# Two-layer decoder trunk on one core: SBUF padded so that matmul operands begin at one place modulo 512 bytes, Strassen sums kept over passes, banks named

## The chip, the core and the metric

The kernel runs on one core of one Trainium2 chip, alone. The metric is the device time of one execution in microseconds. Before the change it is 2031.8 us, the median of three runs (2031.58 to 2032.2).

## What is computed

Two layers over 256 tokens of width 2048, everything in float32. Layer 0 is a gated short convolution, layer 1 multi-head latent attention; each is followed by a squared-ReLU MLP of width 8192, and each half of a layer ends with a normalised residual. Cut to what the change touches:

```python
D_MODEL = 2048; SEQ = 256; DEPTH = 2; D_FF = 4 * D_MODEL
ALPHA = (2 * DEPTH) ** 0.25

def short_conv_mixer(x, w_in, conv_w, w_out):
    bcu = x @ w_in
    gate_b, gate_c, u = jnp.split(bcu, 3, axis=-1)
    v = gate_c * u
    ...
    return (gate_b * y) @ w_out

def sq_relu_mlp(x, w1, w2):
    return jnp.square(jax.nn.relu(x @ w1)) @ w2

for layer in range(DEPTH):
    if layer < N_A:
        mix = short_conv_mixer(h, conv_w_in[layer], conv_w[layer], conv_w_out[layer])
    else:
        ...
        mix = mla_mixer(...)
    h = layer_norm(ALPHA * h + mix, ln_g[layer, 0], ln_b[layer, 0])
    h = layer_norm(ALPHA * h + sq_relu_mlp(h, mlp_w1[layer], mlp_w2[layer]),
                   ln_g[layer, 1], ln_b[layer, 1])
```

## The kernel before

**Numbers in two parts.** A float32 matrix is split into a high and a low part that TensorE multiplies in float32r, three products for one (high x high, high x low, low x high). Weights come from DRAM as raw tiles of 128x1024, on SP's queue; ScalarE copies the high part (L116), VectorE subtracts to get the low part (L117). `take` gives the next weights and prepares those up to five tiles ahead (`LOOK`), so the order of loads, splits and their place among the other work is fixed in the program. An activation tile holds high and low parts side by side.

**Products of 512 columns.** `products` (the MLP's up-projection) and `lagged` (the other wide products) hold a 128x128 block of weights in TensorE and move the activations past it: per 128 rows of the contraction one matmul against 512 columns (L192, high weights against both parts of x) and one against 256 (L196, low weights against x's high part). In the trace's names `out<-moving,held` this is `ps_u<-xhl,hi`. `opening` does the first four products of the kernel in the same way, four banks in turn, in growing runs of chunks. The down-projection is the other way round: `dot` (L276 to L278) holds a 128x128 piece of the hidden activations and moves 512 columns of weights past it, three times.

**The MLP** (`mlp`) runs over the hidden width in eight passes (q = 0 to 7) of eight chunks. A pass computes its eight products of up-projection, whose outputs `hidden` reads out (ScalarE copies one half, VectorE adds the other, L333), squares and splits into `h` (L337, L338). Then come the down-projections of the pass, of four column blocks n of 512 by two halves t of 128 tokens, added up in the SBUF tile `acc` by `put` (copied in pass 0, L577, added later, L581). Pass 0 takes its inputs before the norm is finished and corrects after; pass 7 ends in `to_wide` (layer 0: transposes, L665, and the next norm) or in `to_out` (layer 1: last norm with the vectors `gbt`, and stores).

**Fast passes.** In passes 1 to 6 the column blocks 0 and 1 are done by Strassen's scheme: seven products in place of eight, each of 4 steps of three matmuls, 84 matmuls in all (`down_fast`, tile `ps_f`). Blocks 2 and 3 then take 96 plain matmuls (`down`, `ps_d`). Both layers together have twelve fast passes. The sums of activations that the scheme needs are formed by VectorE (L605 to L608) into the tile `forms`; sums of weights by `prepare` (L149 to L155), the last one in a tile `t4`. After the seven products `combine` folds them into `acc`, with eleven additions by VectorE and a copy by ScalarE, the scratch `vu` being two of the raw tiles.

**Banks.** PSUM has eight banks, taken in turn by every output: four of the pool `pmm`, four of a second pool.

**Places in SBUF.** These are the places at which the built program puts the tiles that TensorE reads, as byte address modulo 512, before and after the change. All lie in the same 128 partitions.

| tile | before | after |
|---|---|---|
| weights, high and low (`hi`, `lo`, and the Strassen sums `hi_t`, `lo_t`) | 384 | 384 |
| `h`, `lat` (tag c) | 384 | 384 |
| `forms`, `kqv` (tag a2) | 0 | 384 |
| `t4` | 256, one buffer | 384, two buffers |
| first input `xhl_a`, chunks 0 to 7 (a1) | 384 | 384 |
| first input `xhl_a`, chunks 8 to 15 (a2) | 0 | 384 |
| `xhl`, `z`, `oT` (tag b) | 128 | 128 |
| `kpe` | 256 | 384 |

In the down-projection `h` and `forms` are held and the weights and `t4` (named `t` in the trace) move; in the other products the weights are held.

Of the kernel before, what the change touches and what calls it, by code (L numbers as in the profile page):

```python
# [16 lines left out]
P = 128  # L17
W = 256 + 2
T = 256
# [31 lines left out]
def trunk(ctx: ExitStack, tc: tile.TileContext, xT, vecs, w_first, w_in, w_out, w_kv, w_q, w_uk, w_uv,  # L51
# [9 lines left out]
    pmm = ctx.enter_context(tc.tile_pool(name="pmm", bufs=4, space=PS))  # L61
# [12 lines left out]
    def mlp_stream(l):  # L74
        out = []
        for q in range(NQ):
            out += halves(w1[l, q * QC:(q + 1) * QC])
            lead = 0
            if q in FAST:
                out += [(w2f[l, q, j, 0], w2f[l, q, j, 1]) for j in range(QC // 2)]  # L80
                lead = 2
            out += halves(w2[l, q, lead:])
        return out
# [6 lines left out]
    class Banks:  # L90
# [4 lines left out]
        @classmethod  # L95
        def open(cls, name):
            st = ExitStack()
            cls.more, cls.count = st.enter_context(tc.tile_pool(name=name, bufs=4, space=PS)), 0
            return st
# [6 lines left out]
        @classmethod  # L106
        def next(cls):
            cls.count += 1
            return cls.more if cls.more is not None and cls.count % 8 >= 4 else pmm
# [70 lines left out]
    def psum(name):  # L180
        return Banks.next().tile([P, 512], F32, tag="mm", name=name)
# [83 lines left out]
    def products(n, x, turned=None):  # L265

        for i in range(n):
            w = take()
            ps = psum("ps_u")
            mm_run([(w, ps)], x, 0, NC, NC, turned=None if i else turned)  # L270
            yield ps
# [8 lines left out]
    def held(x, t):  # L280

        return [x[:, o + t * P:o + (t + 1) * P] for o in (0, T)]
# [5 lines left out]
    def down(x, put, n):  # L288

        ps = [psum("ps_d") for _ in range(2)]  # L290
        for j in range(len(x) // 2):
            w, = take(1)
            for kk in range(2):
                k = 2 * j + kk
                for t in range(2):
                    dot(ps[t], wide_rows(w, kk), held(x[k], t), k == 0, k == len(x) - 1)
        for t in range(2):
# [13 lines left out]


    FACTORS = (("4", "22", "T4"), ("2", "12", "21"), ("3", "S4", "22"), ("1", "11", "11"),
               ("6", "S2", "T2"), ("7", "S3", "T3"), ("5", "S1", "T1"))

    def down_fast(x, forms):

        ps = {p: psum(f"ps_f{p}") for p, _, _ in FACTORS}
        n = len(x) // 2
        for j in range(n):  # L320
            b, = take(1)
            a = {"11": held(x[2 * j], 0), "12": held(x[2 * j + 1], 0), "22": held(x[2 * j + 1], 1)}
            for i in range(4):
                a[f"S{i + 1}"] = [forms[:, j, o, i * P:(i + 1) * P] for o in range(2)]
            for p, l, r in FACTORS:
                dot(ps[p], b[r], a[l], j == 0, j == n - 1)
        return ps
# [14 lines left out]
    cos_t = const.tile([P, T], F32, name="cos_t")  # L342
    sin_t = const.tile([P, T], F32, name="sin_t")
    mask_t = const.tile([P, 3 * P], F32, name="mask_t")
# [9 lines left out]

    def late_constants():
        nc.sync.dma_start(id_t, ident)
        nc.sync.dma_start(cos_t, cosT)
        nc.sync.dma_start(sin_t, sinT)
        nc.sync.dma_start(mask_t, mask)
# [145 lines left out]
    xres = act.tile([P, NC, T], F32, tag="xres", name="xres")  # L505
# [47 lines left out]
    late_constants()  # L553
# [3 lines left out]
    def mlp(idx, ln, blocks, fast, begin=None, extra=None):  # L557
# [24 lines left out]

        for q in range(NQ):
# [5 lines left out]
            if q == NQ - 1 and begin:  # L589
                begin()  # L590
            pair = []

            def hidden(m, ps, evac, *func):
                f = tmp.tile([P, T], F32, tag="fh", name="fh", bufs=3)
# [5 lines left out]
                pair.append(f)  # L600
                if forms is not None and m % 2:
                    (a11, a21), (a12, a22) = ((v[:, :P], v[:, P:]) for v in pair[-2:])
                    sf = fast.tile([P, 4, P], F32, tag="sf", name="sf")
                    s1, s2, s3, s4 = (sf[:, i, :] for i in range(4))
                    nc.vector.tensor_tensor(s1, a21, a22, ALU.add)  # L605
                    nc.vector.tensor_tensor(s3, a21, a11, ALU.subtract)
                    nc.vector.tensor_tensor(s2, s1, a11, ALU.subtract)
                    nc.vector.tensor_tensor(s4, a12, s2, ALU.subtract)  # L608
                    split(forms[:, m // 2, 0, :], forms[:, m // 2, 1, :], sf.rearrange("p i c -> p (i c)"))

            if q == 0:
                for m in range(QC):
# [12 lines left out]
                    if m > 0:  # L625
                        normal()
                acc = act.tile([P, 2, D], F32, tag="a1", name=f"acc{idx}")
            else:
                for m, ps in enumerate(products(QC, xhl, turned=None if q == NQ - 1 and begin else TURNED)):
                    hidden(m, ps, whole)  # L630

# [3 lines left out]
            if q in FAST:  # L635
# [6 lines left out]
    def combine(put, p):  # L642

        put(0, 1, p["4"])
        put(0, 0, p["2"])
        put(1, 0, p["3"])
        v, u = (raws.tile([P, 2, BW], F32, tag="raw", name="vu")[:, i, :] for i in range(2))
        put(0, 0, p["1"])
        nc.scalar.copy(v, p["1"])
        nc.vector.tensor_tensor(v, v, p["6"], ALU.add)  # L650
        nc.vector.tensor_tensor(u, v, p["7"], ALU.add)
        put(1, 0, v)
        put(0, 1, u)
        put(1, 0, p["5"])
        put(1, 1, u)
        put(1, 1, p["5"])
# [23 lines left out]
    def prepare_all():  # L680
        for k in range(NC):
            ln.prepare(k)

    with tc.tile_pool(name="fast1", bufs=1) as fast:
        mlp(1, before, to_wide, fast, begin=prepare_all)


    with tc.tile_pool(name="att", bufs=1) as ap:
        lat = act.tile([P, 2 * NK, 2 * T], F32R, tag="c", name="lat")
        chl, qhl = ([lat[:, k, :] for k in range(o, o + NK)] for o in (0, NK))  # L690
        kpe = ap.tile([P, 2, T], F32, name="kpe")
# [6 lines left out]
        def rope(dst, src, rows):  # L698

            a = tmp.tile([P, T], F32, tag="sq", name="ropea")  # L700
            b = tmp.tile([P, T], F32, tag="nu", name="ropeb")
# [201 lines left out]
    def turn_residual(block, n):  # L903
        if 0 <= n < NB:
            for t in range(2):
                ps = psum("turned")
                for j in range(4):
                    nc.tensor.transpose(ps[:, j * P:(j + 1) * P], xres[:, 4 * n + j, t * P:(t + 1) * P], id_t)
                nc.vector.scalar_tensor_tensor(block(n, t), ps, ALPHA, block(n, t), ALU.mult, ALU.add)

    def to_out(block, put, h):
        gbt = act.tile([P, NB, 2 * BW], F32, tag="b", name="gbt")
        for n in range(NB):
            nc.gpsimd.dma_start(gbt[:, n, :], gb[n].partition_broadcast(P))
# [148 lines left out]
```

## Time and profile before

| what | before |
|---|---|
| median of the runs | 2031.8 us |
| the profiled execution, its own time | 2031.86 us |
| its span | 2030.0 us |
| granted TensorE clock | 1.0 |
| TensorE, VectorE, ScalarE busy | 2022.8, 1637.1, 1186.2 us |
| DMA, mean over the span | 190 GB/s |

The span runs from the first to the last instruction that the profiler saw; the time of an execution has some 2 us more around it. PE is TensorE, PEld its weight loads (they overlap the matmuls), DVE VectorE, ACT ScalarE, POOL GpSimd, SP the engine that issues most DMAs. Matmuls are pipelined: the duration given for one (390 ns for 512 columns) is longer than the distance from its start to the next, so the sum of durations in a group is not its share of the time, and times of stretches are taken from start to start.

### The profile page before, as it was taken

To read this page: it belongs to the slowest core of one execution; us is meant where nothing else is said; L and a number is where in the kernel's file an instruction comes from. 1 tells how busy PE (TensorE), PEld (TensorE's weight loads), DVE (VectorE), ACT (ScalarE), POOL (GpSimd) and SP (SyncE) were. 2 spreads that over 40 slices of the span, in tenths; PEclk is the share of its full clock that TensorE was granted. 3 is DMA by queue.
4 is the path that set the end of the run, shared out by engine and by line. 5 is a ranking of instruction groups with operands and counts; after the bars stand their busy time and mean duration, and the time that the engine had idled before them with its cause. 6 is when DMAs were issued, how large, how long until landed. Compare 5 with 4: busy or idle time off the path is not lost.

```text
span 2030.0 us, 30192 instructions
## 1 busy us (share of the span) xinstructions
PE 2022.8 (100%) x11240; PEld 1763.4 (87%) x11240; DVE 1637.1 (81%) x2559; ACT 1186.2 (58%) x1849; POOL 4.5 (0%) x25
## 2 busy tenths in 40 slices
PE   9999999999999999999999999999999999999998
PEld 8888888988888888888889998898888888888886
DVE  7667677778898988989788978776889898898966
ACT  6444445676566565655656655566656656565661
POOL 0000000000000000000000000000000000000000
PEclk9999999999999999999999999999999999999999
DMA  8666666564746557465654544656474664746573
GB/s 307 209 191 187 188 190 193 162 210 138 251 148 216 193 170 256 145 229 174 232 176 153 177 129 137 195 168 205 136 240 155 213 204 164 250 143 221 190 228 121
DMA packets 106851, 385.32 MB, mean 190 GB/s; under 512 B 11856, under 2 KB 12752, under 8 KB 106448
## 3 DMA queue, kind: packets, MB, share of 16 engines
q1 hardware_dynamic: 105984, 381.17, 57.9%
q0 software_dynamic: 576, 2.10, 0.3%
q8 instruction: 88, 1.44, 0.3%
q14 instruction: 59, 0.48, 0.1%
q10 hardware_dynamic: 144, 0.13, 0.0%
HBM read 381.25 MB, written 2.10 MB: 189 GB/s over the span
## 4 chain that ended last, share of the span: by engine, by line
PE 99%; DMA 0%; DVE 0%; issue 0%; SPq 0%; ACT 0%; DVEq 0%
PE ps_u L192 20%; PE ps_l L192 13%; PE ps_u L196 11%; PE ps_d L276 7%; PE ps_d L277 7%; PE ps_d L278 7%; PE ps_l L196 7%; PE ps_f L278 4%; PE ps_f L276 4%; PE ps_f L277 4%; PE ps_w L226 1%; PE ps_w L224 1%; PE ps_w L225 1%; PE ps_g L226 1%; PE ps_g L224 1%; PE ps_g L225 1%
## 5 line engine op out<-in xcount | busy, mean ns | idle before, releaser
L117 DVE TENSOR_TENSOR lo<-raw,hi 128x1024 fp32r<-128x1024 f32 x710 | 858.7, 1222 | 271.5 <-ACT hi L116 199.9
L116 ACT CAST hi<-raw 128x1024 fp32r<-128x1024 f32 x710 | 740.9, 1050 | 428.4 <-DMA raw<-in_w_dram 134.6
L192 PE MATMUL ps_u<-xhl,hi 128*128 128x512 f32 x1792 | 621.3, 391 | 0.0
L196 PE MATMUL ps_u<-xhl,lo 128*128 128x256 f32 x1792 | 500.1, 280 | 0.0
L192 PEld LDWEIGHTS ps_u<-xhl,hi 128*128 128x128 f32 x1792 | 334.4, 187 | 71.9
L196 PEld LDWEIGHTS ps_u<-xhl,lo 128*128 128x128 f32 x1792 | 339.2, 189 | 1.7
L276 PE MATMUL ps_d<-hi,h 128*128 128x512 f32 x640 | 249.9, 390 | 0.0
L277 PE MATMUL ps_d<-lo,h 128*128 128x512 f32 x640 | 249.3, 390 | 0.0
L278 PE MATMUL ps_d<-hi,h 128*128 128x512 f32 x640 | 249.2, 389 | 0.0
L192 PE MATMUL ps_l<-xhl_a,hi 128*128 128x512 f32 x704 | 244.1, 393 | 0.0
L196 PE MATMUL ps_l<-xhl_a,lo 128*128 128x256 f32 x704 | 195.5, 280 | 0.0
L192 PEld LDWEIGHTS ps_l<-xhl_a,hi 128*128 128x128 f32 x704 | 132.2, 188 | 29.8
L278 PEld LDWEIGHTS ps_d<-hi,h 128*128 128x128 f32 x640 | 120.2, 188 | 25.2
L276 PEld LDWEIGHTS ps_d<-hi,h 128*128 128x128 f32 x640 | 120.2, 188 | 25.0
L277 PEld LDWEIGHTS ps_d<-lo,h 128*128 128x128 f32 x640 | 120.2, 188 | 24.6
L196 PEld LDWEIGHTS ps_l<-xhl_a,lo 128*128 128x128 f32 x704 | 131.9, 188 | 0.2
L597 ACT ACTIVATE fh<-fh 128x256 f32<-128x256 f32 x112 | 46.5, 415 | 89.2 <-DVE fh L333 89.1
L116 ACT CAST hi_t<-raw_t 128x1024 fp32r<-128x1024 f32 x48 | 50.6, 1054 | 55.5 <-DVE raw_t L149 30.5
L192 PE MATMUL ps_l<-z,hi 128*128 128x512 f32 x240 | 82.4, 391 | 0.0
L226 PE MATMUL ps_w<-xd,hi 128*128 128x258 f32 x256 | 72.7, 285 | 0.0
L224 PE MATMUL ps_w<-xd,hi 128*128 128x258 f32 x256 | 72.6, 284 | 0.0
L225 PE MATMUL ps_w<-xd,lo 128*128 128x258 f32 x256 | 72.4, 283 | 0.0
(253 smaller groups left out, 3185.1 us busy)
## 6 DMA issues: line engine op xcount, KB each, us to landing
raw<-in_w_dram SPq DMA_DIRECT2D x416, 512.0 KB, 4.3
raw<-in_w2f_dram SPq DMA_DIRECT2D x96, 512.0 KB, 3.5
raw<-in_w_in_dram SPq DMA_DIRECT2D x88, 512.0 KB, 3.8
raw<-in_w_out_dram SPq DMA_DIRECT2D x32, 512.0 KB, 3.6
raw<-in_w_o_dram SPq DMA_DIRECT2D x32, 512.0 KB, 4.0
raw<-in_w_kv_dram SPq DMA_DIRECT2D x10, 512.0 KB, 3.6
raw<-in_w_q_dram SPq DMA_DIRECT2D x8, 512.0 KB, 4.4
raw<-in_w_uk_dram SPq DMA_DIRECT2D x8, 512.0 KB, 4.6
```

Of the source, the lines that this page charges most:

```text
L116: nc.scalar.copy(hi, src)
L117: nc.vector.tensor_tensor(lo, src, hi.bitcast(F32), ALU.subtract)
L192: nc.tensor.matmul(ps, w[blk // 8][0][:, blk % 8, :], x, start=first, stop=False)
L196: nc.tensor.matmul(ps[:, :T], w[blk // 8][1][:, blk % 8, :], x[:, :T], start=False, stop=last)
L224: nc.tensor.matmul(ps[:, :W], hi, x[k][:, :W], start=k == 0, stop=False)
L225: nc.tensor.matmul(ps[:, :W], lo, x[k][:, :W], start=False, stop=False)
L226: nc.tensor.matmul(ps[:, :W], hi, x[k][:, W:], start=False, stop=k == NC - 1)
L276: nc.tensor.matmul(ps, x[0], w[0], start=first, stop=False)
L277: nc.tensor.matmul(ps, x[0], w[1], start=False, stop=False)
L278: nc.tensor.matmul(ps, x[1], w[0], start=False, stop=last)
L597: nc.scalar.activation(f, f, AF.Relu)
```

## The change

1. Tiles are declared once at the start in a set order with pads between them (`at_...`), so that the held and the moving operands begin where the table above says. The DMA scratch shrinks from 16384 to 4096 bytes to make room.
2. In the fast passes the seven products are no longer folded after each pass. Three of them ("2", "3", "4") are added to their own block of `acc`, four ("1", "5", "7", "6") to a tile `sums`, copied there in the first fast pass; `fold` does the combining once, one step after each of the first products of pass 7.
3. `down_fast` becomes `first_pair` and `fast_products`; the seven factors are taken in another order, and `t4` has two buffers.
4. PSUM banks are named: the up-projection of passes 1 to 7 uses banks 0 and 1 alone, the Strassen products 2 to 7 and 0, the plain blocks 1, 2 and 3, 4, the transposed residual 5 and 6. Other outputs take turns as before.
5. In the fast passes `h` is split for two chunks at once.
6. The next norm's preparation in layer 0, which was done all together at the start of pass 7, takes two chunks after each product of that pass (the first chunk in pass 0). The transposed residual in layer 1 is added between block 2 and block 3, not before block 3's banks are taken.
7. The rotary tables and the mask are loaded on SP's queue behind the first MLP instead of after the convolution; `gbt` is loaded by SP instead of GpSimd.

```diff
-    pmm = ctx.enter_context(tc.tile_pool(name="pmm", bufs=4, space=PS))
+    pmm = ctx.enter_context(tc.tile_pool(name="pmm", bufs=1, space=PS))
+    xres = act.tile([P, NC, T], F32, tag="xres", name="xres")
+    for tag, columns in (("c", 4096), ("pad0", 64), ("b", 8256), ("a1", 4128), ("pad1", 96), ("a2", 4128), ("pad2", 96)):
+        act.tile([P, columns], F32, tag=tag, name=f"at_{tag}")
+    small.tile([P, 32], F32, tag="pad", name="at_pad", bufs=1)
...
-        f = state["fast"].tile([P, 2, BW], F32R, tag="t4", name=f"t4_{i}")
+        f = state["fast"].tile([P, 2, BW], F32R, tag="t4", name=f"t4_{i}", bufs=2)
...
-    def psum(name):
-        return Banks.next().tile([P, 512], F32, tag="mm", name=name)
+    def psum(name, bank=None):
+
+        bank = Banks.next() if bank is None else bank
+        return (pmm if bank < 4 else Banks.more).tile([P, 512], F32, tag=f"mm{bank}", name=name)
...
-    FACTORS = (("4", "22", "T4"), ("2", "12", "21"), ("3", "S4", "22"), ("1", "11", "11"),
-               ("6", "S2", "T2"), ("7", "S3", "T3"), ("5", "S1", "T1"))
-
-    def down_fast(x, forms):
-
-        ps = {p: psum(f"ps_f{p}") for p, _, _ in FACTORS}
-        n = len(x) // 2
-        for j in range(n):
-            b, = take(1)
...
+    OWN, KEPT = ("1", "5", "7", "6"), (2, 3, 4, 5, 6, 7, 0)
+    FACTORS = (("3", "S4", "22"), ("1", "11", "11"), ("5", "S1", "T1"), ("7", "S3", "T3"),
+               ("2", "12", "21"), ("6", "S2", "T2"), ("4", "22", "T4"))
+
+    def fast_products(ps, x, forms, j, n):
+
+        b, = take(1)
+        a = {"11": held(x[2 * j], 0), "12": held(x[2 * j + 1], 0), "22": held(x[2 * j + 1], 1)}
+        for i in range(4):
+            a[f"S{i + 1}"] = [forms[:, j, o, i * P:(i + 1) * P] for o in range(2)]
+        for p, l, r in FACTORS:
+            dot(ps[p], b[r], a[l], j == 0, j == n - 1)
...
+        sums = fast.tile([P, 4, BW], F32, name=f"sums{idx}")
+
+        def keep(p, ps):
+
+            at = sums[:, OWN.index(p)] if p in OWN else block(*{"2": (0, 0), "3": (1, 0), "4": (0, 1)}[p])
+            if q == 0 or q == FAST[0] and p in OWN:
+                nc.scalar.copy(at, ps)
+            else:
+                nc.vector.tensor_tensor(at, at, ps, ALU.add)
...
+        def fold():
+
+            s1, s5, s7, s6 = (sums[:, i] for i in range(4))
+            both = acc[:, 1, :2 * BW].rearrange("p (b c) -> p b c", b=2)
+            right = acc[:, :, BW:2 * BW]
+            two = lambda v: v.unsqueeze(1).to_broadcast([P, 2, BW])
+            for d, a, b in ((block(0, 0), block(0, 0), s1), (s6, s6, s1), (block(1, 0), block(1, 0), s6),
+                            (s7, s7, s6), (both, both, two(s7)), (right, right, two(s5))):
+                nc.vector.tensor_tensor(d, a, b, ALU.add)
+                yield
...
-                put_split(h[m], f)
+                if both is None:
+                    put_split(h[m], f)
+                elif m % 2:
+                    at = ht[:, m - 1:m + 1, :]
+                    split(at[:, :, :T], at[:, :, T:], both)
+                    form(m // 2)
...
+                folds = fold()
+                for m, ps in enumerate(products(QC, xhl, TURNED, (0, 1))):
                     hidden(m, ps, whole)
+                    if q == NQ - 1:
+                        next(folds, None)
+                        if begin:
+                            begin(range(max(2 * m, 1), 2 * m + 2))
...
-            if q in FAST:
-                combine(put, down_fast(h, forms))
-            for n in range(2 if q in FAST else 0, NB):
-                if n == NB - 1 and extra:
-                    extra(block, q - 1)
-                down(h, put, n)
+            if q == 0:
+                for n in range(NB):
+                    down(h, put, n)
+            else:
+                first_pair(h, forms, KEPT)
+                for n, banks in ((2, (1, 2)), (3, (3, 4))):
+                    down(h, put, n, banks)
+                    if extra and n == 2 and q <= NB:
+                        for t in range(2):
+                            extra(block, q - 1, t, 5 + t)
...
-            nc.gpsimd.dma_start(gbt[:, n, :], gb[n].partition_broadcast(P))
+            nc.sync.dma_start(gbt[:, n, :], gb[n].partition_broadcast(P))
...
-    nc = _bacc.Bacc("TRN2", target_bir_lowering=False, num_devices=1)
+    nc = _bacc.Bacc("TRN2", target_bir_lowering=False, num_devices=1, dynamic_dma_scratch_size=4096)
```

More of the change, by code (lines that the diff above doesn't have):

```diff
@@ L77, in mlp_stream @@
             out += halves(w1[l, q * QC:(q + 1) * QC])
-            lead = 0
-            if q in FAST:
-                out += [(w2f[l, q, j, 0], w2f[l, q, j, 1]) for j in range(QC // 2)]
-                lead = 2
-            out += halves(w2[l, q, lead:])
+            plain = halves(w2[l, q, 2:] if q in FAST else w2[l, q])
+            fast = [(w2f[l, q, j, 0], w2f[l, q, j, 1]) for j in range(QC // 2)] if q in FAST else []
+            at = 0 if q or q not in FAST else len(plain) // 2
+            out += plain[:at] + fast + plain[at:]
         return out
@@ L263, in opening, with products @@
         yield from [ps for _, ps in ws]
-    def products(n, x, turned=None):
+    def products(n, x, turned=None, banks=(None,)):
         for i in range(n):
             w = take()
-            ps = psum("ps_u")
+            ps = psum("ps_u", banks[i % len(banks)])
             mm_run([(w, ps)], x, 0, NC, NC, turned=None if i else turned)
@@ L286, in wide_rows, with down @@
         return [v[:, 4 * kk:4 * kk + 4, :].rearrange("p a c -> p (a c)") for v in w]
-    def down(x, put, n):
-        ps = [psum("ps_d") for _ in range(2)]
+    def down(x, put, n, banks=(None, None), amid=None):
+        ps = [psum("ps_d", bank) for bank in banks]
         for j in range(len(x) // 2):
@@ L581, in put, with first_pair @@
                 nc.vector.tensor_tensor(block(n, t), block(n, t), ps, ALU.add)
+        sums = fast.tile([P, 4, BW], F32, name=f"sums{idx}")
[5 more added lines that the diff above has]
+                nc.vector.tensor_tensor(at, at, ps, ALU.add)
+        def first_pair(h, forms, banks):
+            n = QC // 2
+            ps = {p: psum(f"ps_f{p}", bank) for (p, _, _), bank in zip(FACTORS, banks)}
+            for j in range(n):
+                fast_products(ps, h, forms, j, n)
+            for p in ps:
+                keep(p, ps[p])
+        def fold():
[7 more added lines that the diff above has]
+                yield
         for q in range(NQ):
@@ L588, in mlp, with pair_tile, form @@
                 forms = act.tile([P, QC // 2, 2, 4 * P], F32R, tag="a2", name=f"forms{idx}_{q}")
-            if q == NQ - 1 and begin:
-                begin()
             pair = []
+            def pair_tile(m):
+                if m % 2 == 0:
+                    pool = (act, "ab") if m % 4 else (fast, "fp")
+                    t = pool[0].tile([P, 2 * T], F32, tag=pool[1], name="fp")
+                    pair.append(t.rearrange("p (i t) -> p i t", i=2))
+                return pair[-1]
+            def form(j):
+                (a11, a21), (a12, a22) = ((pair[j][:, i, :P], pair[j][:, i, P:]) for i in range(2))
+                sf = fast.tile([P, 4, P], F32, tag="sf", name="sf")
+                s1, s2, s3, s4 = (sf[:, i, :] for i in range(4))
+                nc.vector.tensor_tensor(s1, a21, a22, ALU.add)
+                nc.vector.tensor_tensor(s3, a21, a11, ALU.subtract)
+                nc.vector.tensor_tensor(s2, s1, a11, ALU.subtract)
+                nc.vector.tensor_tensor(s4, a12, s2, ALU.subtract)
+                split(forms[:, j, 0, :], forms[:, j, 1, :], sf.rearrange("p i c -> p (i c)"))
             def hidden(m, ps, evac, *func):
-                f = tmp.tile([P, T], F32, tag="fh", name="fh", bufs=3)
+                both = pair_tile(m) if q in FAST else None
+                f = both[:, m % 2, :] if both is not None else tmp.tile([P, T], F32, tag="fh", name="fh", bufs=3)
                 evac(ps, f, *func)
@@ L678, in trunk, with prepare_chunks @@
     before, ln = ln, Norm(1, ALPHA)
-    def prepare_all():
-        for k in range(NC):
+    def prepare_chunks(chunks):
+        for k in chunks:
             ln.prepare(k)
     with tc.tile_pool(name="fast1", bufs=1) as fast:
-        mlp(1, before, to_wide, fast, begin=prepare_all)
+        mlp(1, before, to_wide, fast, begin=prepare_chunks)
     with tc.tile_pool(name="att", bufs=1) as ap:
@@ L690, in trunk @@
         chl, qhl = ([lat[:, k, :] for k in range(o, o + NK)] for o in (0, NK))
+        cos_t = ap.tile([P, T], F32, name="cos_t")
+        sin_t = ap.tile([P, T], F32, name="sin_t")
+        mask_t = ap.tile([P, 3 * P], F32, name="mask_t")
+        for t, source in ((cos_t, cosT), (sin_t, sinT), (mask_t, mask)):
+            nc.sync.dma_start(t, source)
         kpe = ap.tile([P, 2, T], F32, name="kpe")
```

65 lines of the change are left out of this document (13 added, 52 removed).

## The prediction

> **What bounds the kernel now.** I read the page first: its head, the busy shares, the clock and the chain of waits.
>
> ```profile
> span 2030.0 us, 30192 instructions
> PE 2022.8 (100%) x11240; PEld 1763.4 (87%) x11240; DVE 1637.1 (81%) x2559; ACT 1186.2 (58%) x1849; POOL 4.5 (0%) x25
> PEclk9999999999999999999999999999999999999999
> PE 99%; DMA 0%; DVE 0%; issue 0%; SPq 0%; ACT 0%; DVEq 0%
> ```
>
> TensorE is busy for 2022.8 of 2030.0 us at an ungated clock, and 99% of the chain is its own. Next come its waits, the whole view:
>
> ```profile
> PE offset L961 <- DVE udiag L959: 1.2, 1, 1.2
> PE warm L351 <- DVE col L353: 1.1, 1, 1.1
> PE ps_g L192 <- ACT hi L116: 0.6, 1, 0.6
> PE lnAB L376 <- DVE rr L371: 0.3, 1, 0.3
> ```
>
> They sum to 3.2 us, all at the two ends or in the norm. So there is no wait to remove. Time can only come from the pitch of the matmuls, by which I mean the distance from one start to the next, since the busy time of one overlaps its neighbour. The timeline of TensorE gives it. Columns: start, duration, engine, line, operation, output<-moving,held. This is one fast pass of the first layer:
>
> ```profile
> 584.64 0.39 PE L276 MATMUL ps_f<-t,h 128*128 128x512 f32 x1
> ...
> 604.23 0.40 PE L276 MATMUL ps_d<-hi,h 128*128 128x512 f32 x1
> ...
> 606.08 0.39 PE L278 MATMUL ps_d<-hi,h 128*128 128x512 f32 x1
> ...
> 611.29 0.39 PE L277 MATMUL ps_d<-lo,h 128*128 128x512 f32 x1
> ...
> 625.80 0.39 PE L278 MATMUL ps_d<-hi,h 128*128 128x512 f32 x1
> 626.03 0.39 PE L192 MATMUL ps_u<-xhl,hi 128*128 128x512 f32 x1
> ```
>
> The 84 Strassen matmuls take 604.23 - 584.64 = 19.59 us, 233.2 ns each. The 96 plain ones take 21.80 us; of these the first eight take 1.85 (231 ns each), and the 64 from 611.29 to 625.80 take 14.51, 226.7 ns each. All are 128x128 against 128x512, in float32r, back to back, from one helper. So the same instruction has two pitches, 6.5 ns apart. It is so in each of the twelve fast passes; here is the last, in the other layer:
>
> ```profile
> 1889.85 0.39 PE L276 MATMUL ps_f<-t,h 128*128 128x512 f32 x1
> ...
> 1909.44 0.40 PE L276 MATMUL ps_d<-hi,h 128*128 128x512 f32 x1
> ```
>
> It takes 19.59 us again. A number that steady isn't chance or contention with other engines' traffic, which differs from pass to pass; it belongs to the operands.
>
> **What the addresses have to do with it.** In the addresses of the built program (table above) the plain matmuls read weights at 384 modulo 512 and h at 384. The Strassen ones mix weights at 384 with forms at 0, t4 at 256 with h at 384, and some pairs at 384 on both sides in between. Two other places test the reading. In the opening the held weights are at 384, the moving x at 384 (first half of the chunks, a1) or 0 (second half, a2); in the attention ps_v has 384 on both sides.
>
> ```profile
> 18.04 3.88 PE L192 MATMUL ps_g<-xhl_a,hi 128*128 128x512 f32 x16
> 21.76 2.09 PE L196 MATMUL ps_g<-xhl_a,lo 128*128 128x256 f32 x16
> 29.30 1.98 PE L192 MATMUL ps_l<-xhl_a,hi 128*128 128x512 f32 x8
> 31.12 0.28 PE L196 MATMUL ps_l<-xhl_a,lo 128*128 128x256 f32 x1
> 1187.71 0.39 PE L277 MATMUL ps_v<-lo,lat 128*128 128x512 f32 x1
> ...
> 1191.33 0.40 PE L278 MATMUL ps_v<-hi,lat 128*128 128x512 f32 x1
> ```
>
> Sixteen matmuls from a2 take 21.76 - 18.04 = 3.72 us, 232.5 ns each; eight from a1 take 1.82, 227.5; sixteen of ps_v take 3.62, 226.3. Unlike places give about 233 and like places about 227, in three helpers. I take it that a 512-wide matmul whose held operand is loaded beside it loses a few nanoseconds where the two streams start at different places. Against it stands that the like pairs inside the Strassen run aren't fast either; but they come three or six in a row, and a plain run too needs its first eight to settle (231 against 226.7).
>
> The Trainium skill, "TensorE: Matmul & The Clock Gate", part 2, step-by-step, says otherwise: there are two independent SBUF read ports, and loading the next weights takes no read bandwidth from the running matmul. By that rule a pad changes nothing and the time stays where it is (the second rival). These rows don't bear it out.
>
> **The change part by part.** (1) Fast passes. After it weights, h, forms and both t4 buffers all start at 384, so a fast pass is 84 + 96 = 180 like matmuls in a row. The 84 go from 19.59 us to 84 x 0.2267 = 19.04, with the settling of eight (8 x (231 - 226.7) = 0.04) moved to their front, where the plain run then doesn't pay it: 19.59 + 21.80 = 41.39 becomes 180 x 0.2267 + 0.04 = 40.85, a gain of 0.54. Twelve passes: -6.5 us. Another row of the same thing bounds it: by mean durations of one, at the grouped view,
>
> ```profile
> L276 PE MATMUL ps_d<-hi,h 128*128 128x512 f32 x640 | 249.9, 390 | 0.0
> L276 PE MATMUL ps_f<-hi,forms 128*128 128x512 f32 x96 | 38.1, 397 | 0.0
> L277 PE MATMUL ps_f<-lo,h 128*128 128x512 f32 x96 | 37.7, 392 | 0.0
> ```
>
> the Strassen groups are 2 to 7 ns above the plain ones, so 1008 matmuls are worth -2.0 to -7.1 us; I take the pitch, since it needs no model of the ends.
>
> (2) The short convolution's input product. Its a2 half moves from 0 to 384 beside held weights at 384. Steady pairs (a 512-wide and a 256-wide matmul) of it and of the next product, whose z is at 128:
>
> ```profile
> 266.66 0.39 PE L192 MATMUL ps_l<-xhl_a,hi 128*128 128x512 f32 x1
> ...
> 270.14 0.39 PE L192 MATMUL ps_l<-xhl_a,hi 128*128 128x512 f32 x1
> ...
> 275.48 0.39 PE L192 MATMUL ps_u<-z,hi 128*128 128x512 f32 x1
> ...
> 279.64 0.39 PE L192 MATMUL ps_u<-z,hi 128*128 128x512 f32 x1
> ```
>
> Ten pairs take 3.48 us, 348.0 ns; twelve take 4.16, 346.7. 704 pairs are worth 0 to -0.9; I take -0.5, the middle, as only one part of each pair comes from a2. The opening gives 32 x (232.5 - 226.7) = -0.2. The up-projection keeps 128 against 384, so its 1792 pairs gain nothing: this is why the whole is small.
>
> (3) VectorE's work. Each fast pass had eleven 512-wide additions that fold the seven products (nine at L581, of which six read ps_f and three the scratch vu, and L650 and L651). Now it has seven accumulations, of which four are copies on ScalarE in the first fast pass: 38 a layer, and one fold of six in the last pass. Rows, by form:
>
> ```profile
> L581 DVE TENSOR_TENSOR acc<-acc,ps_f 128x512 f32<-128x512 f32 x72 | 48.1, 682 | 0.4
> L581 DVE TENSOR_TENSOR acc<-acc,vu 128x512 f32<-128x512 f32 x36 | 23.7, 686 | 0.0
> L651 DVE TENSOR_TENSOR vu<-vu,ps_f 128x512 f32<-128x512 f32 x12 | 8.3, 688 | 1.2
> L338 DVE TENSOR_TENSOR h<-fh,h 128x256 fp32r<-128x256 f32 x128 | 53.7, 421 | 2.2 <-ACT h L337 1.5
> L117 DVE TENSOR_TENSOR lo<-raw,hi 128x1024 fp32r<-128x1024 f32 x710 | 858.7, 1222 | 271.5 <-ACT hi L116 199.9 <-issue 48.2 <-PE ps_l L196 18.3
> ```
>
> That is 48.1 + 23.7 + 2 x 8.3 = 88 us before and about 2 x 38 x 0.685 = 52 plus two folds (four of 0.69 and two of twice the width, which I put at the 1.22 of L117, 5.2 each) after, 62 in all; splitting h in pairs makes of eight at 0.42 four near 0.69, another 0.6 x 12 = 7. VectorE has some 33 us less to do. On the path it is worth nothing: TensorE waits for none of it. If the cover were gone, the 0.69 us of one addition would be its price.
>
> (4) Named banks. The up-projection turns over two banks instead of eight, so the high part of product m+2 waits until product m is read out, at most one product later: 16 x 346.7 = 5.55 us. The latest read-out I found:
>
> ```profile
> 830.77 0.28 PE L196 MATMUL ps_u<-xhl,lo 128*128 128x256 f32 x1
> ...
> 834.45 0.42 DVE L333 TENSOR_TENSOR fh<-ps_u,t 128x256 f32<-128x256 f32 x1
> ```
>
> It ends at 834.87, 3.8 us after the product's end at 831.05. The product between began 0.12 after the first row, at 830.89, and would end at 836.44: 1.6 us are left. In the last pass of layer 0 the fold and two chunks of the norm's preparation now stand behind each product's work and so ahead of the next read-out: 0.69 or 1.22 and two of 0.42, 1.5 to 2.1 us against the 1.6, if it met the latest read-out. Waiting there on VectorE's queue would be the next read-out and the weights' low parts behind it. Two folds are the wide ones, so I put 0 to +1 us, together with the turn of the banks to the transposes after layer 0, and take +0.1, because most read-outs come earlier than this one.
>
> (5) gbt goes from GpSimd's queue to SP's, behind it the last weights; it must wait for the last read of xhl either way.
>
> ```profile
> L914 POOL DMA_DIRECT2D gbt<-in_gb_dram x4: 527/529/662, 1976.1 to 1977.8; - x4
> L931 DVE TENSOR_TENSOR acc<-acc,gbt x3: 687/690/691, 1989.8 to 2017.5; 128x512 f32<-128x512 f32 x3
> raw<-in_w_dram SPq DMA_DIRECT2D x416, 512.0 KB, 4.3
> ```
>
> On SP the last four weight loads stand behind the waiting issues, and TensorE's last plain products wait for those. They can start no earlier than 1976.1 and four issues of 0.53, land 4.3 later, at about 1983, and serve the last column block, which comes well after the 1989.8 at which the first block's gbt is used. Price: nothing, at worst one landing of 4.3 if the landings queue up behind gbt's. The rotary tables and the mask leave the start of SP's queue and are loaded behind the first MLP's fold, ahead of the attention: nothing. The attention's own a2 tile moves to 384 as well; its matmuls are narrower or fp32, and I give them 0 to -0.3 and take nothing.
>
> The sum: -6.5 - 0.5 - 0.2 + 0.1 = -7.1, off the profiled execution's 2031.86 us (span 2030.0): 2024.8. The median of the runs shown is 2031.8, 0.06 lower, so 2024.7.
>
> **The rivals.** First, part of it only: what settles the pitch is one stream's run of like places, and changing the moving operand at every product (plain runs use each twice) keeps some of the loss. For it: the like pairs in Strassen runs are slow now. Against it: ps_v, whose moving operand changes with each step. At half the gain, -3.5: 2028.3. Second, the place doesn't matter: seven sums taking turns in seven banks, or their order, make the 233 ns, and the pads do nothing. Against it: the opening takes turns over four banks in both its halves and shows both pitches. It leaves 2031.8 less 0 to 0.7. That is also how it goes if the pads fall elsewhere than meant. Third, slower: read-outs of the up-projection late by two weight subtractions. Two are 2.44 us, against 1.6 in hand: 0.85 on each product behind which it happens. With three in each of the fourteen passes that is +36, less 7.1: 2061; it outweighs the gain from nine such waits on, and the two banks leave it nowhere to go. Against it: VectorE has less to do than before, and the order of subtraction and read-out in its stream is kept.
>
> **How the numbers follow.** Forecast 0.80, half of it 0.08, no effect 0.07, two banks 0.05. Its own bounds: all -7.1 of the grouped view, -0.9 and -0.2 give 2023.7, and ps_v's 226.3 instead of 226.7 in all 2160 matmuls another -0.9, 2022.8; the half reaches 2028.4. So 2022.8 to 2028.4 holds forecast and most of the half. A measurement tells 0.2% from none, 4.06 us: faster is under 2027.7, which has the forecast and half of the second case, 0.80 + 0.04 = 0.84; same 0.04 + 0.07 = 0.11; slower 0.05.
>
> **What would show it.** In the timeline the distance from the first ps_f to the first ps_d of a pass should be 19.1 us instead of 19.59, and that from there to the next ps_u 21.76. Sixteen matmuls of the opening from a2 should take 3.63 instead of 3.72. The waits of TensorE should hold no ps_u row. If ps_f stays at 233 ns the address reading is wrong; if ps_f falls but the span doesn't, look at the waits of ps_u and at the first matmuls of each pass.

## The result, and the profile after

The changed kernel takes 2026.51 us (median of ten runs, 2026.02 to 2028.61), the kernel before 2032.03 (ten runs beside them). The ratio is 0.9975, 95% interval 0.9966 to 0.9984: 5.5 us less. The forecast was 2024.7, 7.1 less, with 2022.8 to 2028.4 as its range. So the direction and most of the amount came, and 1.6 us of it did not.

The page of the changed kernel: its head, busy shares and chain of waits, and then the whole view of TensorE's waits.

```profile
span 2026.4 us, 30052 instructions
PE 2018.3 (100%) x11240; PEld 1763.1 (87%) x11240; DVE 1605.8 (79%) x2467; ACT 1176.2 (58%) x1797; POOL 2.3 (0%) x21
PE 99%; DMA 0%; DVE 0%; SPq 0%; issue 0%; ACT 0%; DVEq 0%
```

```profile
PE ps_g L199 <- ACT hi L121: 1.9, 1, 1.9
PE offset L998 <- DVE udiag L996: 1.2, 1, 1.2
PE warm L355 <- DVE col L357: 1.1, 1, 1.1
```

As before, TensorE is 99% of the chain, with the same 11240 matmuls. VectorE has 31.3 us less work. There is no wait for the up-projection's two banks. Line numbers have shifted: the wide products are L199 and L203, `dot` is L283 to L285.

The pass that the prediction showed, in TensorE's timeline (start, duration, engine, line, operation, output<-moving,held):

```profile
587.70 0.39 PE L283 MATMUL ps_f<-hi,forms 128*128 128x512 f32 x1
...
606.78 0.39 PE L283 MATMUL ps_d<-hi,h 128*128 128x512 f32 x1
...
628.54 0.39 PE L199 MATMUL ps_u<-xhl,hi 128*128 128x512 f32 x1
```

The 84 Strassen matmuls take 606.78 - 587.70 = 19.08 us, the 96 plain ones 21.76, 40.84 in all against 41.39. That is the forecast to 0.01 us. Each of the twelve passes saves 0.54 or 0.55: -6.6 us.

What did not come is in a place where the prediction had put nothing, the convolution's output product over z:

```profile
289.90 0.40 PE L199 MATMUL ps_l<-z,hi 128*128 128x512 f32 x1
...
300.50 0.40 PE L199 MATMUL ps_l<-z,hi 128*128 128x512 f32 x1
```

There are 30 pairs of a 512-wide and a 256-wide matmul between these two starts: 10.60 us, 353.3 ns a pair. In the kernel before, 30 pairs of z took 10.40 us, 346.7 ns each, from operands at the same places modulo 512:

```profile
289.25 0.39 PE L192 MATMUL ps_l<-z,hi 128*128 128x512 f32 x1
...
299.65 0.39 PE L192 MATMUL ps_l<-z,hi 128*128 128x512 f32 x1
```

From its first matmul to the next product all 256 pairs of z take 90.43 us instead of 88.79: +1.6 us, about what is missing.

The profiled execution itself took 2028.49 us, 2 us over the median, and two of the ten runs did so. Its opening shows why. The view of windows gives the busy times in a stretch, then the granted clock, DMA share and GB/s:

```profile
12.00:32.00 20.00, 20.00 (x109) 17.62 (x109) 15.43 (x26) 13.88 (x26) 0.00 (x0) 0.92 0.96 369
```

In this stretch of the opening the clock was 0.92, and 1.9 us were waited for the first weights instead of 0.6. In the same kernel's second trace, below, the clock is 1.00 and that wait 1.0 us.

### The profile page after: what moved, and what is told of

It is laid out like the page before. It is cut to its first block, busy times and chain, and to the rows that moved or that the text cites. A ratio compares the mean times of both kernels' runs of the same rounds, so it can differ in the third digit from the quotient of the medians.

```text
span 2026.4 us, 30052 instructions
## 1 busy us (share of the span) xinstructions
PE 2018.3 (100%) x11240; PEld 1763.1 (87%) x11240; DVE 1605.8 (79%) x2467; ACT 1176.2 (58%) x1797; POOL 2.3 (0%) x21
## 4 chain that ended last, share of the span: by engine, by line
PE 99%; DMA 0%; DVE 0%; SPq 0%; issue 0%; ACT 0%; DVEq 0%
PE ps_u L199 20%; PE ps_l L199 13%; PE ps_u L203 11%; PE ps_d L285 7%; PE ps_d L283 7%; PE ps_d L284 7%; PE ps_l L203 7%; PE ps_f L284 4%; PE ps_f L285 4%; PE ps_f L283 4%; PE ps_w L233 2%; PE ps_w L231 2%; PE ps_w L232 2%; PE ps_g L231 1%; PE ps_g L233 1%; PE ps_g L232 1%
## 5 line engine op out<-in xcount | busy, mean ns | idle before, releaser
L199 PE MATMUL ps_u<-xhl,hi 128*128 128x512 f32 x1792 | 621.0, 391 | 0.0
L203 PE MATMUL ps_u<-xhl,lo 128*128 128x256 f32 x1792 | 499.5, 280 | 0.0
L199 PEld LDWEIGHTS ps_u<-xhl,hi 128*128 128x128 f32 x1792 | 334.2, 187 | 72.4
L203 PEld LDWEIGHTS ps_u<-xhl,lo 128*128 128x128 f32 x1792 | 338.6, 189 | 1.8
L283 PE MATMUL ps_d<-hi,h 128*128 128x512 f32 x640 | 249.8, 390 | 0.0
L285 PE MATMUL ps_d<-hi,h 128*128 128x512 f32 x640 | 249.1, 389 | 0.0
L199 PE MATMUL ps_l<-xhl_a,hi 128*128 128x512 f32 x704 | 243.5, 392 | 0.0
L203 PE MATMUL ps_l<-xhl_a,lo 128*128 128x256 f32 x704 | 194.8, 279 | 0.0
L199 PEld LDWEIGHTS ps_l<-xhl_a,hi 128*128 128x128 f32 x704 | 131.7, 187 | 29.5
L283 PEld LDWEIGHTS ps_d<-hi,h 128*128 128x128 f32 x640 | 120.2, 188 | 25.0 <-DVE fh L340 0.3
L285 PEld LDWEIGHTS ps_d<-hi,h 128*128 128x128 f32 x640 | 120.1, 188 | 24.9
L203 PEld LDWEIGHTS ps_l<-xhl_a,lo 128*128 128x128 f32 x704 | 132.2, 188 | 0.2
L199 PE MATMUL ps_l<-z,hi 128*128 128x512 f32 x240 | 83.9, 398 | 0.0
L641 ACT ACTIVATE fp<-fp 128x256 f32<-128x256 f32 x96 | 40.0, 416 | 72.6 <-DVE fp L340 71.9
```

The costliest lines, as they stand in the source:

```text
L199: nc.tensor.matmul(ps, w[blk // 8][0][:, blk % 8, :], x, start=first, stop=False)
L203: nc.tensor.matmul(ps[:, :T], w[blk // 8][1][:, blk % 8, :], x[:, :T], start=False, stop=last)
L283: nc.tensor.matmul(ps, x[0], w[0], start=first, stop=False)
L285: nc.tensor.matmul(ps, x[1], w[0], start=False, stop=last)
```

## The experiments

**The same kernel again.** No edit.

> The changed kernel once more, for a second trace. In its first profiled execution (2028.49 us) the Strassen stretch of a fast pass fell to 19.08 us as forecast, but two stretches were longer than before: the opening (by 2.3 us, with a granted clock of 0.92 in its first 20 us) and the convolution's output product over z (by 1.6 us, 353.3 ns for a pair of matmuls in place of 346.7). Theory Z (z's rhythm belongs to this program: it is set by the way in which the run is entered): z again 353 ns a pair, every time. Rival (an accident of that execution, as the opening): z at 346.7 here. Both: the opening's 2.3 us is an accident of single executions, so a usual execution takes 2026.4 us and its opening is within 0.3 us of before.

Measured: 2026.22 us (7 runs), profiled 2026.23. The same window of the opening, and the same stretch of z:

```profile
12.00:32.00 20.00, 20.00 (x116) 17.61 (x115) 17.00 (x27) 15.49 (x27) 0.00 (x0) 1.00 0.92 362
```

```profile
288.77 0.40 PE L199 MATMUL ps_l<-z,hi 128*128 128x512 f32 x1
...
299.37 0.40 PE L199 MATMUL ps_l<-z,hi 128*128 128x512 f32 x1
```

The opening's loss is gone. z stays slow: 30 pairs take 10.60 us again. Summed from start to start, the 512-wide matmuls of its 240 pairs behind the first product take 56.63 us, against 55.22 before and 56.76 in the first trace. So z's loss belongs to the program and the opening's to single executions.

**Pads alone, in the kernel before.**

```diff
+    for tag, columns in (("a1", 4096), ("pad1", 96), ("a2", 4128), ("pad2", 32)):
+        act.tile([P, columns], F32, tag=tag, name=f"at_{tag}")
...
         state["fast"] = fast
+        fast.tile([P, 32], F32, tag="pad", name=f"at_pad{idx}")
```

> The kernel before with nothing but pads: a2 (second half of the first input, forms) and t4 begin at 384 modulo 512, like the weights and h; order of work, banks, folds as before. Theory A (the places of the held and moved operands set the pitch): each Strassen stretch of 84 goes from 19.59 to 19.08 us, the whole to 2024.5 to 2026.5 us (the upper end if z's pairs take 353 ns here too). Rival B (banks, factor order or the folds made the gain): 19.59 us, 2031 to 2032 us.

Measured: 2026.45 us (9 runs), ratio 0.9972 (0.9962 to 0.9982). The Strassen stretch of the same pass:

```profile
585.20 0.39 PE L276 MATMUL ps_f<-t,h 128*128 128x512 f32 x1
...
604.28 0.39 PE L276 MATMUL ps_d<-hi,h 128*128 128x512 f32 x1
```

It takes 19.08 us, and so do the other eleven. z is slow here too (90.3 us from its first start to its last, against 88.7 before). So the pads alone make the whole result, and they bring z's loss with them. Named banks, sums kept over passes and the other order of work are not needed for either.

**The places of before, in the changed kernel.**

```diff
-("a1", 4128), ("pad1", 96), ("a2", 4128), ("pad2", 96)
+("a1", 4128), ("a2", 4128), ("pad2", 192)
...
         sums = fast.tile([P, 4, BW], F32, name=f"sums{idx}")
+        fast.tile([P, 96], F32, tag="pad", name=f"at_pad{idx}")
```

> The changed kernel with the places of before for forms and the second half of the first input (0 modulo 512) and for one t4 buffer pair (256); everything else as changed. Theory A: Strassen stretches back at 19.5 to 19.7 us, the whole at 2031 to 2033 us. Rival B: 19.08 us and 2026.5 us stay.

Measured: 2030.24 us (11 runs), ratio 0.999 (0.9982 to 0.9999).

```profile
585.26 0.39 PE L283 MATMUL ps_f<-hi,forms 128*128 128x512 f32 x1
...
604.75 0.39 PE L283 MATMUL ps_d<-hi,h 128*128 128x512 f32 x1
```

Each Strassen stretch takes 19.49 us and z's pairs 346.7 ns. The gain is gone for the most part, as theory A has it, but the whole is 0.8 us below its lower end. The traces show where most of that is: at the same unlike places the kernel before took 19.59, 0.1 us more a stretch, 1.3 in twelve. The order of the factors, the banks and the second `t4` buffer differ between the two, and no run tells which of them it is. With like places both take the same 19.08.

**z at the place of its weights.**

```diff
-    zt = act.tile([P, NC, 2 * T], F32R, tag="b", name="z")
+    zt = act.tile([P, 8256], F32R, tag="b", name="z")[:, 64:].rearrange("p (k c) -> p k c", k=NC)
```

> The changed kernel with z alone moved by 256 bytes, from 128 to 384 modulo 512, the place of the weights that are held beside it. Theory Z with places (unequal places allow a slow and a fast rhythm, equal ones only the fast): z's pairs at 346.5 to 346.7 ns, the whole 1.5 to 1.8 us less than the changed kernel, 2024.7 to 2025.0. Rival (z is slow for another reason, such as traffic beside it or its base address): 353 ns, no gain.

Measured: 2026.01 us (7 runs).

```profile
288.83 0.40 PE L199 MATMUL ps_l<-z,hi 128*128 128x512 f32 x1
...
299.43 0.40 PE L199 MATMUL ps_l<-z,hi 128*128 128x512 f32 x1
```

Thirty pairs of z still take 10.60 us, 353.3 ns each. My theory that unlike places let the slow pitch in fell with this run. What was left: in every trace so far z was slow where both halves of the run before it, over the first input, lay at one place, and fast where they lay at two. That run changes its own pitch on the way, at a spot that the timeline of the changed kernel shows:

```profile
160.61 0.59 PE L394 MATMUL mu0p<-xres,ones 128*128 128x256 f32 x2
160.85 0.58 PE L199 MATMUL ps_l<-xhl_a,hi 128*128 128x512 f32 x1
161.27 0.28 PE L203 MATMUL ps_l<-xhl_a,lo 128*128 128x256 f32 x1
161.38 0.40 PE L199 MATMUL ps_l<-xhl_a,hi 128*128 128x512 f32 x1
```

Here the norm puts a matmul of another kind, with plain float32 operands, into the stream. Before it the starts were 230 and 116.7 ns apart in turn, behind it 231.7 and 115.0 on the average, up to the end of the input's product. So a run of matmuls seems to have more than one rhythm, and to keep the one into which it falls. That became theory E.

**The first input at two places again, forms left where they are.**

```diff
-    xts = [act.tile([P, NC // 2, 2 * T], F32R, tag=a, name=f"xhl0_{a}") for a in ("a1", "a2")]
+    xts = [act.tile([P, 4128], F32R, tag=a, name=f"xhl0_{a}")[:, o:o + 4096].rearrange("p (k c) -> p k c", k=NC // 2)
+           for a, o in (("a1", 0), ("a2", 32))]
```

> The changed kernel with the second half of the first input back at 0 modulo 512 (forms stay at 384). z kept its slow rhythm when its own place was changed, and was fast in every trace in which the first input had two places. Theory E (z's rhythm is handed on from the run before it, which with both halves of the input at one place goes over to pairs of 231.7 and 115 ns at 160 us): z's pairs at 346.7 ns, so -1.6 us, the input's pairs back to 347.5, +0.6, opening +0.1; the whole 1.0 us less than the changed kernel, 2025.3. Rival (the base addresses or the other work during z): 353 ns in z and 0.6 us more than the changed kernel, 2027.0.

Measured: 2025.38 us (5 runs), ratio 0.9967 (0.9955 to 0.998).

```profile
288.80 0.39 PE L199 MATMUL ps_l<-z,hi 128*128 128x512 f32 x1
...
299.20 0.39 PE L199 MATMUL ps_l<-z,hi 128*128 128x512 f32 x1
```

z's pairs take 346.7 ns, though nothing of z, its weights or its work was touched. It is the number that theory E gave. That the norm's matmul at 160 us is what turns the rhythm is read from the trace; no run takes it out.

**One pair exchanged at z's entry.**

```diff
-    summed(ln, chain(products(1, z), lagged(NC - 1, z)), residual)
+    summed(ln, chain(products(1, z, TURNED), lagged(NC - 1, z)), residual)
```

> The changed kernel with one pair of matmuls of z's first product exchanged (low before high at the third chunk, as all up-projections have it). Theory E (a rhythm is entered and kept): an exchange near the entry can set another rhythm; z's pairs at 346.7 ns and the whole 1.5 us less, 2024.8. Rival (z's rhythm belongs to its operands and place): 353 ns, no change.

Measured: 2024.84 us (5 runs, 2024.52 to 2025.35), ratio 0.9965 (0.9951 to 0.9978). The same stretch of z's timeline:

```profile
289.81 0.39 PE L199 MATMUL ps_l<-z,hi 128*128 128x512 f32 x1
...
300.21 0.39 PE L199 MATMUL ps_l<-z,hi 128*128 128x512 f32 x1
```

Thirty pairs in 10.40 us, 346.7 ns. The order of two of the 11240 matmuls is worth 1.4 us, because it sets the rhythm of the some 250 pairs that follow.

**The opposite: no exchange at the up-projections.**

```diff
-                for m, ps in enumerate(products(QC, xhl, TURNED, (0, 1))):
+                for m, ps in enumerate(products(QC, xhl, None, (0, 1))):
```

> The changed kernel without the exchanged pair of matmuls at the start of each up-projection. Theory E (a rhythm is entered and kept): the up-projections enter from a run of 512-wide matmuls in the order in which z did; where they enter the slow rhythm, 128 pairs a pass cost 6.6 ns each, 0.85 us a pass, up to 12 us in fourteen passes, 2027 to 2038 us. Rival (only z is liable to it): no change, 2026.2 us.

Measured: 2037.97 us (8 runs), ratio to the kernel before 1.0028 (1.0018 to 1.0039). Thirty pairs of the up-projection with the exchange (the changed kernel), and then without:

```profile
649.71 0.39 PE L199 MATMUL ps_u<-xhl,hi 128*128 128x512 f32 x1
...
660.11 0.39 PE L199 MATMUL ps_u<-xhl,hi 128*128 128x512 f32 x1
```

```profile
649.91 0.40 PE L199 MATMUL ps_u<-xhl,hi 128*128 128x512 f32 x1
...
660.51 0.40 PE L199 MATMUL ps_u<-xhl,hi 128*128 128x512 f32 x1
```

10.40 and 10.60 us, 346.7 and 353.3 ns a pair, and the slow one in all fourteen passes. 1792 pairs by 6.6 ns are 11.8 us; measured are 11.5 against the first ten runs of the changed kernel and 11.8 against the seven of the second set. A detail of the kernel before fits this: its last pass of layer 0 has no exchange, yet was fast. There the norm's matmul stands at the entry and may set the rhythm, which no run tests by itself:

```profile
968.92 0.40 PE L278 MATMUL ps_d<-hi,h 128*128 128x512 f32 x1
969.15 0.59 PE L396 MATMUL mu0p<-xres,ones 128*128 128x256 f32 x2
969.40 0.59 PE L192 MATMUL ps_u<-xhl,hi 128*128 128x512 f32 x1
```

The change moved that matmul to pass 0 and gave this pass the exchange.

**Sixteen distances.** The tiles of the tags b, c and a2 were made longer, and each pass begins `h` and `forms` at another offset within them (cut to `h` and `xhl`; `forms` goes like `h`):

```diff
+    PLACE = ((0, 32, 64, 96, 128, 160, 192, 224), (256, 288, 320, 384, 448, 480, 16, 4))
...
+            o = PLACE[idx // 2][q] // 4
+            ht = act.tile([P, 4224], F32R, tag="c", name=f"h{idx}_{q}")[:, o:o + 4096].rearrange("p (k c) -> p k c", k=QC)
...
+        o = {1: 96, 3: 112}[idx]
+        xt = act.tile([P, 8320], F32R, tag="b", name=f"xhl{idx}")[:, o:o + 8192].rearrange("p (k c) -> p k c", k=NC)
```

> The changed kernel, with h and forms of each MLP pass begun at another distance from the weights' place (0, 32, 64, 96, 128, 160, 192, 224 bytes in the passes 0 to 7 of the first layer, 256, 288, 320, 384, 448, 480, 16 and 4 in the second), and the four tiles of tag b at four distances (z 0, xhl of the first MLP 128, oT 256, xhl of the second 192). One look, read pass by pass from start to start. Theory A as the prediction had it (a loss wherever the places differ modulo 512): 226.7 ns in ps_d and 19.08 us for 84 ps_f at distance 0 alone, 229 to 234 ns and 19.2 to 19.6 us elsewhere. Theory A' (only part of the distance counts, such as halves of 512): 256 like 0. Theory A'' (only distances that are no multiple of some smaller step cost): a good pitch at most multiples of 64 or 128. The up-projection's pair: 346.7 ns whatever the distance, since it showed that at 256 and the first input at 0 and 384.

Measured, one run: 2048.87 us, 22.4 more than the changed kernel, with the same work and no new wait. The plain stretches of four passes, at 32, 128, 192 and 16 bytes:

```profile
520.53 0.40 PE L283 MATMUL ps_d<-hi,h 128*128 128x512 f32 x1
...
542.93 0.39 PE L199 MATMUL ps_u<-xhl,hi 128*128 128x512 f32 x1
...
781.43 0.39 PE L283 MATMUL ps_d<-hi,h 128*128 128x512 f32 x1
...
803.73 0.40 PE L199 MATMUL ps_u<-xhl,hi 128*128 128x512 f32 x1
...
954.81 0.39 PE L283 MATMUL ps_d<-hi,h 128*128 128x512 f32 x1
...
976.79 0.40 PE L199 MATMUL ps_u<-xhl,hi 128*128 128x512 f32 x1
...
1924.53 0.39 PE L283 MATMUL ps_d<-hi,h 128*128 128x512 f32 x1
...
1946.29 0.39 PE L199 MATMUL ps_u<-xhl,hi 128*128 128x512 f32 x1
```

Each is 96 matmuls: 22.40, 22.30, 21.98 and 21.76 us. All passes read in this way, from start to start (ns for one 512-wide matmul of `ps_d`; passes 0 and 7 have 192). The distance is the held operand's place less the moving one's:

| distance, bytes | 0 | 4 | 16 | 32 | 64 | 96 | 128 | 160 | 192 | 224 |
|---|---|---|---|---|---|---|---|---|---|---|
| ns | 227.9 | 232.3 | 226.7 | 233.3 | 233.3 | 234.3 | 232.2 | 233.3 | 229.0 | 234.6 |
| distance + 256 | 256 | | | 288 | 320 | | 384 | | 448 | 480 |
| ns | 226.8 | | | 234.1 | 234.2 | | 233.2 | | 229.8 | 233.3 |

The 0 is that of a pass 0, which starts from another kind of run; in the fast passes of the changed kernel it is 21.76 / 96 = 226.7. The passes with 224, 288, 320, 384 and 448 have transposes between their plain blocks, and there the changed kernel too has more, 228.8 at the 224 and 227.8 at the others. Against the same pass of the changed kernel the losses are 6.6 and 6.3 ns at 32 and 288, 6.6 and 6.4 at 64 and 320, 5.5 and 5.4 at 128 and 384, 2.3 and 2.0 at 192 and 448, 5.8 and 6.6 at 224 and 480. So the second line repeats the first: what counts is the distance modulo 256, not 512. It is good at 0, and at 16 in the one pass that had it; 192 costs about 2 ns, all the rest 5 to 8.

One rival stays open. The weights begin at 384 in every run, so every pair at distance 0 has both operands at 128 modulo 256. The runs don't tell whether the distance counts or whether each operand is fast at that place by itself.

For the up-projection the two distances that are new modulo 256 cost too: 351.0 ns a pair at 384 and 353.2 at 320 (the expectation counts them the other way round, as 128 and 192), against 346.7 at 256 in the changed kernel. It is so in all seven passes of a layer, whatever the place of the run ahead. 353.2 is also the pitch of the slow rhythm, so it isn't known whether the place costs this by itself or lets the run fall into that rhythm in spite of the exchange. Theory A' holds, and the expectation that the up-projection doesn't care was wrong: its 256 had been a like place all along.

**Pads and the exchange, nothing else of the change.** The edit of the second experiment and that of the exchange at z together.

> The kernel before with the pads alone and with the exchanged pair of matmuls in z's first product; no named banks, kept sums or other order. Theory A+E (places and z's rhythm are all that moves the time): z's pairs at 346.7 ns, 1.5 us less than with the pads alone, 2024.8 to 2025.1 us, the same as the changed kernel with that exchange (2024.84). Rival (kept sums and fewer additions are worth something by themselves): over 2025.5.

Measured: 2024.87 us (5 runs, 2024.68 to 2025.25), ratio 0.9963 (0.995 to 0.9975); the changed kernel with the exchange had 2024.84. So the kept sums, the named banks and 31 us less on VectorE are worth nothing that these runs can tell. These two are the fastest of all the kernels here.

## Why the prediction came out as it did

1. **TensorE's pitch is the bound.** Right. The matmuls are the same 11240 and the waits hold no new row. From the kernel before to the second trace the span falls by 5.9 us: fast passes -6.57, first input -0.61, opening -0.09, z +1.64, all else -0.27.
2. **The Strassen stretches, -6.5 us.** Right in mechanism and size: 40.84 us a pass where 40.85 was forecast. That places alone do it, without banks and order, was argued before and is shown by the kernel with pads alone. One witness was weaker than it seemed: the eight matmuls at 29.30, whose 227.5 ns stood for like places in the opening. They come from `lagged` and write one bank, so they say nothing of four banks in turn; the opening's own runs of eight from a1 took 1.84 us, 230 ns, in the kernel before:

```profile
15.25 2.00 PE L192 MATMUL ps_g<-xhl_a,hi 128*128 128x512 f32 x8
17.09 1.12 PE L196 MATMUL ps_g<-xhl_a,lo 128*128 128x256 f32 x8
```

In the changed kernel's second trace the eight of `lagged`, at the same places, take 29.20 to 31.05, 231 ns each; the sixteen from a2 stand here too:

```profile
18.07 3.82 PE L199 MATMUL ps_g<-xhl_a,hi 128*128 128x512 f32 x16
21.73 2.08 PE L203 MATMUL ps_g<-xhl_a,lo 128*128 128x256 f32 x16
29.20 2.00 PE L199 MATMUL ps_l<-xhl_a,hi 128*128 128x512 f32 x8
31.05 0.28 PE L203 MATMUL ps_l<-xhl_a,lo 128*128 128x256 f32 x1
```

The rule of the Trainium skill that stood against it ("TensorE: Matmul & The Clock Gate", part 2, step-by-step: two independent read ports, so that loading the next weights takes no read bandwidth from the running matmul) does not cover this. With nothing but places changed, 96 matmuls took 21.76 or 22.40 us. It isn't known whether the ports are the reason.
3. **"Places modulo 512".** Half wrong. The step is too strict: 256 is the period. By that rule the up-projection, at a distance of 256, was paying all along; but its pairs take the same 346.7 ns as the first input's do at distance 0 (231.7 + 115.0), and more at 320 and 384. It did no harm to the sum, since the change left that distance alone and the term was nothing either way, which is luck.
4. **The first input's product, -0.5, and the opening, -0.2.** The first is right: in the second trace the input's pairs take 0.6 us less (81.62 + 162.66 against 82.63 + 162.26). The opening gave 0.13 of its 0.2: from the first matmul over a2 to its end it takes 18.07 to 29.20, 11.13 us, against 18.04 to 29.30, 11.26. Sixteen of its wide matmuls over a2 take 3.66 us by the rows above, where 3.63 was forecast.
5. **z, taken as unchanged.** This step failed. I used z's 346.7 ns as the fixed mark against which the input's product was measured, and gave z itself no term: its operands keep their places, so I took its pitch to be kept. The pitch isn't a function of a matmul's own operands alone. It depends on the rhythm that the stream has when the run begins, and the pads altered that rhythm upstream, in the first input. The missing term measures 90.43 - 88.79 = +1.6 us, and -7.1 + 1.6 = -5.5 is what was measured. That it comes out to the tenth is partly luck: the second set of runs, 2032.07 and 2026.22, has -5.85.
6. **VectorE's work is hidden.** Right: 31.3 us less (33 forecast), and the two kernels with the exchange differ by 0.03 us.
7. **Two banks, 0 to +1 us.** Right at its lower end: nothing. In the first trace of the changed kernel the latest read-out ended 3.6 us after its product's end, against some 5.4 until the end of the next. The rival that put the loss there never came near.
8. **gbt and the tables on SP's queue.** No wait showed up, as forecast.

## What to carry to other kernels

Where TensorE never waits, read the pitch from start to start and compare like instructions: 227 and 233 ns for the same matmul were 6.6 us here, and a pad of a few hundred bytes took them back. Begin the held and the moving operand at one place modulo 256 bytes (here 128; no other common place was tried), and time each run of matmuls by itself, since a run can keep a slow rhythm that it took over at its entry. After any edit upstream look again at runs that the edit doesn't touch; a single exchanged pair near the entry, a cheap thing to try, moved two stretches between 346.7 and 353.3 ns a pair.

## What the runs showed that I had not expected

A stream of alternating 512-wide and 256-wide matmuls has at least two steady rhythms with the same operands, 346.7 and 353.3 ns a pair, and stays in one for 128 pairs a pass or all of z's 256. One exchanged pair near the entry of the run can set it, and a matmul of another kind seems to; an exchange of the same kind that `lagged` makes later within z left the slow rhythm in place. Why one exchange decides and another doesn't, and why 192 bytes is better than 128, stays open: the runs show that it is so, and no more. The tolerance of 16 bytes rests on one pass, and so does the loss at 4. The cost of an unlike place isn't the same in every stream either: the 352 pairs of the first input that read a2 lost 0.6 us at a distance of 384, 1.7 ns each, and the up-projection's pairs 4.3.
